# A diffusion backbone step on one core: the first feed-forward's way down by half products, two conditioning vectors moved to TensorE, and x added in the middle sweeps

## The chip, the cores and the metric

The kernel runs on 1 core of one Trainium2 chip. The metric is device microseconds of that core; the median of 3 runs before the change is 2879.01 us (2872.47 to 2881.43).

## What is computed

One layer of a hybrid backbone, for 1024 latent tokens and 128 context tokens with the same weights. All tensors are float32.

```python
def trunk_layer(x, mod, cache, lb, norm_g, ffn1, ffn2, mixer_w):
    m = [mod[:, i][:, None, :] for i in range(N_MOD)]
    x = x + 0.5 * m[2] * swiglu(modulate(x, norm_g[0], m[0], m[1]), *ffn1)
    mix, ctx = token_mixer(modulate(x, norm_g[1], m[3], m[4]), cache, lb, *mixer_w)
    x = x + m[5] * mix
    x = x + 0.5 * m[8] * swiglu(modulate(x, norm_g[2], m[6], m[7]), *ffn2)
    return x, ctx
```

`swiglu(h, w1, w3, w2)` is `(silu(h @ w1) * (h @ w3)) @ w2`, with 1024 model columns and 2816 hidden ones. The token mixer runs attention (8 heads) and a two-way scan side by side. The nine vectors `m` come from `silu(c) @ w_ada + b_ada`, one row for the latent tokens and one for the context; after the change `m[6]` and `m[7]` (shift and scale of the second feed-forward) are computed in another place.

## The kernel before, in words

**Layout.** The 1152 tokens lie along the free axis, the model's columns as 8 tiles `x[0..7]` of 128 x 1152, the hidden columns as 22 blocks `f` of 128. A float32 product is made of three matmuls in a rounded format: every operand is split into a high and a low part, ACT casts the high part, DVE or POOL subtracts to get the low one, and `hi*hi + hi*lo + lo*hi` is summed in PSUM (`mm3`, lines 473 to 475).

**Order of the stages.** Start; first way up (4 plain blocks, then 18 fast blocks); first way down; scan; attention; merge; second way up (3 plain blocks, 19 fast ones); second way down with the final norm. Instructions are issued in the order in which the generators are pulled, and a scheduler then orders each engine's queue. DMAs are issued by SP, in order.

**Fast blocks** (`fast_block`, L1746 its matmuls) compute a block of the way up with seven half-size products instead of eight, 288 tokens wide. Per block there are 2 x 7 x 4 x 3 = 168 matmuls. In them `ada_sum` works in the background: it computes vectors of `m` on DVE (L318), from a weight tile and a row broadcast over the partitions, vectors 2 to 5 in the first way up and 8 in the second.

**First way down** (`ffn_fast` with l = 0). The 22 hidden blocks are read back from HBM (`hs`), split into `hh` and `hl`, and multiplied two at a time: `down_group` (matmuls in `down`, L473 to L475, 384 tokens wide; L502 adds the scaled result to `x`), and the last four in `down_last`, which also starts the next norm. `x` was loaded before. In the background, `self.bg` runs `ada_sum` for the vectors 6 and 7, 64 DVE products in all.

**Second way down** (l = 1, `down_fast`). Sixteen hidden blocks are taken as 8 pairs in three groups of 2, 3 and 3 pairs. In the fast blocks `pair_sums` (L1783 to L1786) has made the seven sums of each pair and written them to HBM (`xd`), and `pair_weights` has made the sums of the weights on POOL and written them to `wsum`, for all but the last three sweeps. A group runs four sweeps `m` (`down_sweep`, L1946 its matmuls, 288 tokens wide); a sweep makes seven products in the order `PRODUCTS`, each for two halves of the tokens: 84 matmuls with two pairs, 126 with three. `down_ops` loads the weights, sums them where `own` holds (L1879, on POOL: four instructions, with the results `ws` twice, `raw` and `wr`), and splits them (ACT L1884, DVE L1885, tiles `wd`), six products ahead. `down_xs` loads the sums of the next group (`xr`, SP L1900, five raw tiles in flight) and splits them (ACT L1910; the low part, L1911, on DVE for the second pair and on POOL for the others) into tiles `xd`; it is pulled in the last sweep of the group before, one group of tiles per product. PSUM is drained by DVE into `su` (L1951) and `x` (L1931, L1933) and by ACT. The first group writes `x` afresh; in each sweep of the second and third group one tile of the old `x` is loaded and added by DVE in two halves (L1991).

**Attention** (`heads`, `block`) runs 16 blocks of nine key tiles. The PSUM tag `mx` (two banks) holds row maxima (L1411, L1412), queries, keys and values.

**Start.** `ada_pe` computes the vectors 0 and 1 on TensorE: per 128 rows of weights four matmuls, each 32 columns of the array wide, side by side (L263), then two transposes (L278).

Of the kernel before, what the change touches and what calls it, by code (L numbers as in the profile page):

```python
# [32 lines left out]
G = 32  # L33
# [12 lines left out]
GROUPS = (3, 2), (7, 3), (13, 3)  # L46
# [47 lines left out]
class Trunk:  # L94
# [27 lines left out]
    def start(self):  # L122
        nc, a, pp = self.nc, self.a, self.pp
        self.sc = self.fp.tile([P, KT, 32], F32, name="sc")
# [130 lines left out]
    def ada_pe(self, m, buf, pin=lambda i: i):  # L255
# [20 lines left out]
        pt = self.pp.tile([P, 2, P], F32, tag="ps1", bufs=1, name="adat")  # L276
# [8 lines left out]
        self.ada_end(m)  # L285

# [344 lines left out]
    def mixer_consts(self):  # L631
        nc, a, cp = self.nc, self.a, self.cp
        self.mask = cp.tile([P, 4, G], U8, name="mask")
        mf = self.tt(F32, "maskf")[:, : 4 * G]
        nc.sync.dma_start(mf, a["mask"])
        nc.vector.tensor_copy(self.mask.rearrange("p a b -> p (a b)"), mf)
# [3 lines left out]
        nc.vector.memset(self.onesb[64:128, 64:128], 1.0 / 64)  # L640
        self.onesq = cp.tile([P, P], F32, name="onesq")
# [490 lines left out]
    def heads(self, qn, ck, ckc, KT_, ktc, rope, w0, sums):  # L1132
# [36 lines left out]
        clear_v(Vs[1])  # L1169
        self.pend, self.mo = [], [None] * 8  # L1170
        pre = self.preload()
        for h in range(H):
# [19 lines left out]
        for _ in pre:  # L1192
# [599 lines left out]
    def pair_weights(self, w2):  # L1792

        nc = self.nc
        self.wsum = self.dp.tile([sum(n for _, n in GROUPS), P, KT // 2, 4, P], F32, name="wsum")
        n = sum(n for _, n in GROUPS)
        for j in range(n):
            f = GROUPS[0][0] + 2 * j
# [18 lines left out]
    def down_ops(self, w2):  # L1817
# [8 lines left out]
        def load(u, key):  # L1826
# [3 lines left out]
            j, f = sum(v for _, v in GROUPS[:g]), GROUPS[g][0]  # L1830
            own = g == len(GROUPS) - 1 and m > 0
# [28 lines left out]
        for u, (g, n, m) in enumerate(units):  # L1860
            load(u + 1, 6)
            load(u + 1, 2)
            if g == len(GROUPS) - 1 and m:
                a11, a21, a12, a22 = [nxt[u, i] for i in (6, 7, 2, 4)]
                s1, s2 = [
                    self.fp.tile([P, CW], F32, tag="hf", bufs=self.hfb, name="ws").rearrange("p (k d) -> p k d", k=n)
# [23 lines left out]
    def down_xs(self, g, X):  # L1890

        nc = self.nc
        j0 = sum(n for _, n in GROUPS[:g])
# [73 lines left out]
    def down_fast(self, w2, X, xg, ops, made, load_x, load_h, split_h, gm, nxt):  # L1967

        S = [self.tt(F32, "su")[:, :T].rearrange("p (m n) -> p m n", m=4) for _ in range(2)]
        rest = [2, *range(PLAIN[1] + 16, NF)]  # L1970
        pend, ws = [], []
        self.folds = []
        for g, (f, n) in enumerate(GROUPS):
            new = {} if g else X
            last = g == len(GROUPS) - 1
            for m in range(KT // 2):
# [38 lines left out]
        assert not self.folds  # L2015
        self.down_group(w2, fs, hs, gm, ws)
# [5 lines left out]
    def ffn_fast(self, l, gm, nxt):  # L2022
# [5 lines left out]
        self.puts, self.ticks, self.roles = [], 0, {}  # L2028
        if l:
# [256 lines left out]
```

## Time and profile before

| | |
|---|---|
| median of 3 runs | 2879.01 us |
| the profiled execution | 2879.34 us |
| its span | 2877.4 us |
| PE busy | 2781.1 us (97%) |
| DVE busy | 2026.9 us (70%) |
| ACT busy | 1332.1 us (46%) |
| POOL busy | 967.3 us (34%) |
| HBM traffic | 331.76 MB, 115 GB/s |

PE is TensorE's matmuls, PEld its weight loads, DVE VectorE, ACT ScalarE, POOL GpSimd, SP the queue that issues DMAs. Times in rows are microseconds from the span's start, a mean or a median marked ns is of one instruction. A row of a group of instructions ends with the idle time of the engine ahead of them and what ended it; a row of waits has the total, the number and the longest. In a row of stretches each engine has its busy time and, in brackets, its number of instructions; then come TensorE's granted clock as a share, the DMA engines' busy share and GB/s.

### The profile page before, as it was taken

Reading aid. Unit: us, or ns where it says so; the run is one execution under the profiler, and the core shown is the slowest. Engines: PE = TensorE matmul, PEld = TensorE weight load, DVE = VectorE, ACT = ScalarE, POOL = GpSimd, SP = SyncE. Lnnn points to the kernel's source line nnn. Section 1 sums busy time; section 2 is a strip of 40 time slices with the busy share of each in tenths; the row PEclk is TensorE's granted clock in tenths of the full one; section 3 lists DMA queues with packets and bytes.
Section 4 is the critical chain, followed back from the end, with each engine's and each line's share of the span. In section 5 each row is a group of like instructions: output and inputs, shape, how many; then the busy total and the mean of one; then the engine's idle time right before and its main releaser. Section 6 shows DMA issues by size and latency. Waiting matters only on the chain. (4 is left out here: it accounts for less than half of the span.)

```text
span 2877.4 us, 55665 instructions
## 1 busy us (share of the span) xinstructions
PE 2781.1 (97%) x21138; PEld 2642.6 (92%) x21138; DVE 2026.9 (70%) x4425; ACT 1332.1 (46%) x2738; POOL 967.3 (34%) x1005
## 2 busy tenths in 40 slices
PE   6999999999999999999999999989999999999998
PEld 5999999999999998988998787779989999999997
DVE  7677777577778777877355777756675666558885
ACT  6432322321166677667535777730552222236332
POOL 0133233354222222222144444532452433424450
PEclk9999999999999999999999999999999999999999
DMA  6644343663121111112412001262553443447631
GB/s 237 203 148 128 125 124 117 214 208 118 61 84 55 50 57 37 57 41 74 162 58 84 18 14 30 72 219 84 178 172 97 157 147 126 134 144 212 198 102 67
DMA packets 218941, 331.76 MB, mean 115 GB/s; under 512 B 24049, under 2 KB 142769, under 8 KB 218673
## 3 DMA queue, kind: packets, MB, share of 16 engines
q1 hardware_dynamic: 218672, 328.20, 35.4%
q8 instruction: 167, 2.74, 0.4%
q14 instruction: 102, 0.83, 0.1%
HBM read 244.93 MB, written 83.18 MB: 114 GB/s over the span
## 5 line engine op out<-in xcount | busy, mean ns | idle before, releaser
L1746 PE MATMUL b<-xo,wo 128*128 128x288 f32 x3552 | 482.0, 295 | 0.0
L1746 PEld LDWEIGHTS b<-xo,wo 128*128 128x128 f32 x3552 | 474.3, 188 | 0.0
L1746 PE MATMUL b<-bh,wo 128*128 128x288 f32 x1776 | 365.0, 295 | 1.2 <-ACT et L1756 1.2
L473 PE MATMUL mm<-xh,wh 128*128 128x384 f32 (+1 forms) x1008 | 351.8, 349 | 10.9 <-DVE sg L750 6.1
L474 PE MATMUL mm<-xl,wh 128*128 128x384 f32 (+1 forms) x1008 | 341.9, 339 | 0.0
L475 PE MATMUL mm<-xh,wl 128*128 128x384 f32 (+1 forms) x1008 | 341.4, 339 | 0.0
L1746 PEld LDWEIGHTS b<-bh,wo 128*128 128x128 f32 x1776 | 288.6, 188 | 1.4 <-ACT et L1756 1.4
L502 DVE SCALAR_TENSOR_TENSOR x<-dn,modt,x 128x256 f32<-128x256 f32 (+4 forms) x472 | 225.6, 499 | 86.9 <-PE dn L475 86.2
L1746 PE MATMUL b<-bl,wo 128*128 128x288 f32 x888 | 261.4, 294 | 0.0
L473 PEld LDWEIGHTS mm<-xh,wh 128*128 128x128 f32 (+1 forms) x1008 | 189.6, 188 | 21.0 <-DVE sg L750 8.3
L1720 ACT CAST wo<-raw 128x512 fp32r<-128x512 f32 x185 | 114.9, 622 | 180.1 <-issue 77.2
L474 PEld LDWEIGHTS mm<-xl,wh 128*128 128x128 f32 (+1 forms) x1008 | 189.3, 188 | 2.3 <-issue 0.7
L475 PEld LDWEIGHTS mm<-xh,wl 128*128 128x128 f32 (+1 forms) x1008 | 189.1, 188 | 1.0
L1946 PE MATMUL d<-xd,wd 128*128 128x288 f32 x1344 | 181.8, 297 | 7.4 <-DVE x L1933 5.4
L1946 PEld LDWEIGHTS d<-xd,wd 128*128 128x128 f32 x1344 | 180.0, 190 | 9.0 <-ACT wd L1884 3.6
L1721 DVE TENSOR_TENSOR wo<-raw,wo 128x512 fp32r<-128x512 f32 x185 | 128.4, 695 | 64.5 <-ACT wo L1720 61.8
L318 DVE SCALAR_TENSOR_TENSOR junk<-wada,cb 128x512 bf16<-128x512 f32 x224 | 163.4, 729 | 12.6 <-DMA wada<-in_w_aT 11.8
L1461 POOL TENSOR_TENSOR ehl<-e,ehl 128x512 fp32r<-128x512 f32 x93 | 122.1, 1317 | 140.6 <-ACT ehl L1459 75.8
L1746 PEld LDWEIGHTS b<-bl,wo 128*128 128x128 f32 x888 | 167.0, 188 | 0.0
L247 POOL TENSOR_TENSOR wl<-raw,wh 128x1024 fp32r<-128x1024 f32 (+3 forms) x51 | 101.2, 1986 | 174.3 <-ACT wh L246 162.3
L1721 DVE TENSOR_TENSOR wo<-ws,wo 128x512 fp32r<-128x512 f32 x74 | 71.2, 962 | 113.4 <-ACT wo L1720 113.2
L1720 ACT CAST wo<-ws 128x512 fp32r<-128x512 f32 x74 | 45.7, 618 | 227.5 <-POOL ws L1716 227.3
(441 smaller groups left out, 7202.6 us busy)
## 6 DMA issues: line engine op xcount, KB each, us to landing
raw<-in_w SPq DMA_DIRECT2D x148, 256.0 KB, 3.5
wada<-in_w_aT SPq DMA_DIRECT2D x112, 256.0 KB, 3.2
raw<-in_w SPq DMA_DIRECT2D x42, 512.0 KB, 4.0
raw<-in_w_in SPq DMA_DIRECT2D x41, 512.0 KB, 3.5
xr<-xd SPq DMA_DIRECT2D x56, 288.0 KB, 3.7
hr<-hs SPq DMA_DIRECT2D x26, 576.0 KB, 5.9
hb<-hd SPq DMA_DIRECT2D x44, 288.0 KB, 3.4
hs<-et SPq DMA_DIRECT2D x84, 144.0 KB, 2.2
```

The source lines that it names most:

```text
L247: pin((eng or self.nc.gpsimd).tensor_sub(wl, raw, wh))
L318: nc.vector.scalar_tensor_tensor(junk, ws[n % 2], 1.0, cs[s], ALU.mult, ALU.mult, accum_out=o)
L473: pin(nc.tensor.matmul(ps, wh, xh, start=start and i == 0, stop=False))
L474: pin(nc.tensor.matmul(ps, wh, xl, start=False, stop=False))
L475: pin(nc.tensor.matmul(ps, wl, xh, start=False, stop=stop and i == n - 1))
L502: nc.vector.scalar_tensor_tensor(self.x[m][:, a:b], ps[:, a - lo : b - lo], self.modt[:, gm, m, s : s + 1], self.x[m][:, a:b], ALU.mult, A ...
L1461: eng.tensor_sub(el, e, eh)
L1720: nc.scalar.copy(wh, src[i])
L1721: nc.vector.tensor_sub(wl, src[i], wh)
L1746: nc.tensor.matmul(ps, w[:, k], x[:, k, :QW], start=first, stop=last, skip_group_check=home != i)
L1946: nc.tensor.matmul(ps, w[:, k], xv, start=start, stop=stop, skip_group_check=home != i)
```

## The change

The first way down goes through `down_fast` too, with the first of its pairs at hidden block 4 (`self.plain`); the groups are now given from there. So the first way up makes the pair sums for 16 blocks and writes them as `xd` instead of `hs`. No `pair_weights` runs for it: `early` makes every sweep of the first way down sum its own weights on POOL. Blocks 0 to 3, 20 and 21 are still multiplied plainly, behind the groups. The vectors 6 and 7 are no longer computed by `ada_sum` in the first way down, but by a new `ada_fill` in attention, two rows of weights at a time: 8 matmuls into an `mx` bank, summed by DVE, and two transposes per vector; it is pulled at two places of each block from the second head on. In both ways down, the old `x` is loaded and added two tiles per sweep, in the code of the second and third sweep of the second and third group; the scheduler puts some of it ahead of them. The constants of the mixer are made in the second group of the first way down, and `sc`, the operand of the conditioning products, moves to a pool that lives through the kernel.

```diff
-GROUPS = (3, 2), (7, 3), (13, 3)
+GROUPS = (0, 2), (4, 3), (10, 3)
+PAIRED = 16
...
+    def ada_fill(self):
+
+        nc, a = self.nc, self.a
+        for m in (6, 7):
+            acc = self.fp.tile([P, 256], F32, tag="ada", bufs=1, name="adar")
+            for k in range(0, KT, 2):
+                w = [self.tt(F32, "wada")[:, :D] for _ in range(2)]
+                for i in range(2):
+                    nc.sync.dma_start(w[i], a["w_ada"][(k + i) * P : (k + i + 1) * P, m * D : (m + 1) * D])
+                yield
+                ps = self.pp.tile([P, 256], F32, tag="mx", bufs=2, name="adap")
+                for i in range(2):
+                    for g in range(4):
+                        v = slice(32 * g, 32 * g + 32)
+                        nc.tensor.matmul(
+                            ps[v, :],
+                            self.sc[:, k + i, :],
+                            w[i][:, 256 * g : 256 * g + 256],
...
+                if k:
+                    nc.vector.tensor_add(acc, ps, acc)
+                else:
+                    nc.vector.tensor_copy(acc, ps)
+                yield
+            self.ada_turn(m, acc, "mx", 2)
+            yield
...
+                    if h and t in (3, 7):
+                        next(fill, None)
...
-    def down_ops(self, w2):
+    def down_ops(self, w2, early):
...
-            own = g == len(GROUPS) - 1 and m > 0
+            own = early or (g == len(GROUPS) - 1 and m > 0)
...
-        rest = [2, *range(PLAIN[1] + 16, NF)]
+        rest = [*range(2, self.plain), *range(self.plain + PAIRED, NF)]
...
-                if g:
-                    xa.append((4 * g - 4 + m, load_x(4 * g - 4 + m)))
+                if g == 1 and m:
+                    next(consts, None)
+                if g and m in (1, 2):
+                    xa += [(i, load_x(i)) for i in range(4 * g + 2 * m - 6, 4 * g + 2 * m - 4)]
...
-                    if xa and k == 3:
-                        i, t = xa.pop()
+                    if xa and k in (2, 5):
+                        i, t = xa.pop(0)
...
-        dops, dmade, X = (self.down_ops(w2) if l else None), [], {}
-        xg = self.down_xs(0, X) if l else None
+        dops, dmade, X = self.down_ops(w2, l == 0), [], {}
+        xg = self.down_xs(0, X)
...
-            self.bg = self.ada_sum((6, 7), lambda: self.bank("up", "cb", D // 2), partial(self.tt, F32), self.slim)
-        if l:
-            self.down_fast(w2, X, xg, dops, dmade, load_x, load_h, split_h, gm, nxt)
-            return
-        for f in range(2, NF):
-            pend.append(split_h(*load_h(f)))
-            if f % 2 and f < NF - 1:
-                fs, hs = zip(*pend[:2])
-                self.down_group(w2, fs, hs, gm, ws or [load_w2(v) for v in fs])
-                pend, ws = pend[2:], None
-        for _ in self.bg:
-            pass
-        fs, hs = zip(*pend)
-        self.down_last(w2, fs, hs, gm, nxt)
+        self.down_fast(w2, X, xg, dops, dmade, load_x, load_h, split_h, gm, nxt)
```

Three places show how the engines' queues move. Line numbers in the rows of the changed kernel are its own; "128x576" is a shape, and "x25" behind it means 25 such instructions in a row.

POOL, where the second way down before the change goes from its first group over the second to the third (the splits `xd` of all three groups stand in these rows):

```order
L1716 TENSOR_TENSOR raw<-raw,ws 128x256 x2
L1911 TENSOR_TENSOR xd<-xr,xd 128x576 x25
L1879 TENSOR_TENSOR ws<-raw,wr 128x384
L1879 TENSOR_TENSOR raw<-raw 128x384
L1911 TENSOR_TENSOR xd<-xr,xd 128x576 x6
```

And POOL in the first way down of the changed kernel, at the change from the first group to the second (L1954 is the split, L1922 the sum of weights):

```order
L1954 TENSOR_TENSOR xd<-xr,xd 128x576
L1922 TENSOR_TENSOR ws<-ws,raw 128x384
L1954 TENSOR_TENSOR xd<-xr,xd 128x576
L1922 TENSOR_TENSOR wr<-wr,ws 128x256
L1922 TENSOR_TENSOR ws<-raw,wr 128x384
L1954 TENSOR_TENSOR xd<-xr,xd 128x576
L1922 TENSOR_TENSOR raw<-raw 128x384
L1954 TENSOR_TENSOR xd<-xr,xd 128x576 x5
L1922 TENSOR_TENSOR ws<-ws,raw 128x384
L1954 TENSOR_TENSOR xd<-xr,xd 128x576 x2
L1922 TENSOR_TENSOR wr<-wr,ws 128x384
L1954 TENSOR_TENSOR xd<-xr,xd 128x576 x4
```

Before, 14 splits of that change of groups stand in an unbroken row; now six sums stand among the 14. At the next change four sums stand among the splits where three stood.

PE in attention before the change, in the fourth pass of row maxima (`mtr` turns them, `po` are the products with the values, `sps` the scores):

```order
L1418 MATMUL mtr<-ident,m_18845 1x128 x4
L1428 MATMUL po<-ehl,V 128x512
L1429 MATMUL po<-ehl,V 128x512
L1430 MATMUL po<-ehl,V 128x512
L1452 MATMUL sps<-qh_17836,kth_17721 128x512
```

And the same place in the changed kernel:

```order
L1459 MATMUL mtr<-ident,m_19381 1x128 x4
L1469 MATMUL po<-ehl,V 128x512
L1470 MATMUL po<-ehl,V 128x512
L1471 MATMUL po<-ehl,V 128x512
L306 MATMUL adap<-wada,sc 32x256 x8
L1493 MATMUL sps<-qh_18367,kth_18252 128x512
```

Eight conditioning matmuls now stand between two key tiles; there are eight such places.

DVE in the second way down, first sweep of the third group, before the change (`x_29906` and `x_29905` are two tiles of x, `d` a PSUM bank):

```order
L1885 TENSOR_TENSOR wd<-ws,wd 128x384
L1933 SCALAR_TENSOR_TENSOR x_29906<-d_31794,modt,x_29906 128x288
L1991 TENSOR_TENSOR x_29906<-x_31706,x_29906 128x576
L1933 SCALAR_TENSOR_TENSOR x_29906<-d_31805,modt,x_29906 128x288
L1885 TENSOR_TENSOR wd<-raw,wd 128x384
L1991 TENSOR_TENSOR x_29906<-x_31706,x_29906 128x576
```

And in the same sweep of the changed kernel (`x_30560` and `x_30559` are the same two tiles of x, L1928 splits weights, L1976 drains PSUM into x, L2037 adds the old x):

```order
L1928 TENSOR_TENSOR wd<-ws,wd 128x384
L1976 SCALAR_TENSOR_TENSOR x_30560<-d_32418,modt,x_30560 128x160
L1976 SCALAR_TENSOR_TENSOR x_30560<-d_32418,modt,x_30560 128x128
L2037 TENSOR_TENSOR x_30560<-x_32549,x_30560 128x576
L1976 SCALAR_TENSOR_TENSOR x_30560<-d_32429,modt,x_30560 128x288
L1928 TENSOR_TENSOR wd<-wr,wd 128x384
L1976 SCALAR_TENSOR_TENSOR x_30560<-d_32396,modt,x_30560 128x288
L1976 SCALAR_TENSOR_TENSOR x_30559<-d_32446,modt,x_30559 128x288
L2037 TENSOR_TENSOR x_30560<-x_32549,x_30560 128x576
```

Before, the two halves stood between the drains of the sweep's fourth product; now they stand between those of its sixth. Of the group's other three tiles of old x, one is added at the end of the second sweep and two in the third; before, one was added in each of the last three sweeps.

More of the change, by code (lines that the diff above doesn't have):

```diff
@@ L275, in ada_pe, with ada_turn @@
         nc.scalar.copy(row, ps)
-        pt = self.pp.tile([P, 2, P], F32, tag="ps1", bufs=1, name="adat")
+        self.ada_turn(m, row, "ps1", 1)
+    def ada_turn(self, m, row, tag, bufs):
+        nc = self.nc
+        pt = self.pp.tile([P, 2, P], F32, tag=tag, bufs=bufs, name="adat")
         for q in range(2):
@@ L1794, in pair_weights @@
         nc = self.nc
-        self.wsum = self.dp.tile([sum(n for _, n in GROUPS), P, KT // 2, 4, P], F32, name="wsum")
-        n = sum(n for _, n in GROUPS)
+        n = PAIRED // 2
+        self.wsum = self.dp.tile([n, P, KT // 2, 4, P], F32, name="wsum")
         for j in range(n):
-            f = GROUPS[0][0] + 2 * j
+            f = self.plain + 2 * j
             for m in range(KT // 2 if j < n - GROUPS[-1][1] else 1):
@@ L1892, in down_xs @@
         nc = self.nc
-        j0 = sum(n for _, n in GROUPS[:g])
+        j0 = GROUPS[g][0] // 2
         units = [(i, k) for i in PRODUCTS for k in range(GROUPS[g][1])]
@@ L2015, in down_fast @@
         assert not self.folds
+        for _ in consts:
+            pass
         self.down_group(w2, fs, hs, gm, ws)
@@ L2027, in ffn_fast @@
         self.hs = self.dp.tile([NF, P, T], F32, name=f"hs{l}")
-        self.puts, self.ticks, self.roles = [], 0, {}
-        if l:
-            self.xd = self.dp.tile([sum(n for _, n in GROUPS), P, 7, 2, QW], F32, name="xd")
-            self.roles = {f + v: (j, v % 2) for j, f in enumerate(range(GROUPS[0][0], PLAIN[1] + 16, 2)) for v in range(2)}
+        self.puts, self.ticks, self.bg = [], 0, iter(())
+        self.plain = plain
+        self.xd = self.dp.tile([PAIRED // 2, P, 7, 2, QW], F32, name="xd")
+        self.roles = {plain + f: (f // 2, f % 2) for f in range(PAIRED)}
         sums, ops, made = iter(()), iter(()), []
```

49 lines of the change are left out of this document (20 added, 29 removed).

## The prediction

> **What bounds the kernel now.** The page comes first: who is busy, and at what clock.
>
> ```profile
> span 2877.4 us, 55665 instructions
> PE 2781.1 (97%) x21138; PEld 2642.6 (92%) x21138; DVE 2026.9 (70%) x4425; ACT 1332.1 (46%) x2738; POOL 967.3 (34%) x1005
> ...
> PEclk9999999999999999999999999999999999999999
> ```
>
> TensorE is busy for 97% of the span at almost the full clock. So a matmul taken away counts fully where PE runs without a gap, and a matmul added counts fully there too; work on the other engines counts only where PE waits for it. The next view is busy time by stage, because the change touches four stages: the fast blocks on the way up, both ways down, and attention.
>
> ```profile
> core 0: us, PE busy (x) PEld busy (x) DVE busy (x) ACT busy (x) POOL busy (x), PEclk, DMA share, GB/s
> 180.00:540.00 360.00, 360.00 (x2720) 360.00 (x2720) 262.69 (x591) 109.43 (x217) 106.52 (x129) 1.00 0.40 126
> 560.00:780.00 220.00, 220.00 (x1255) 219.82 (x1254) 171.42 (x414) 41.15 (x40) 96.35 (x39) 1.00 0.42 147
> 600.00:660.00 60.00, 60.00 (x343) 60.00 (x343) 47.29 (x115) 15.46 (x15) 28.61 (x12) 1.00 0.44 149
> 1560.00:1800.00 240.00, 238.26 (x1153) 191.97 (x1152) 173.94 (x330) 185.34 (x354) 115.86 (x101) 1.00 0.08 22
> 2460.00:2520.00 60.00, 60.00 (x456) 60.00 (x455) 35.82 (x68) 16.82 (x36) 24.05 (x38) 1.00 0.38 119
> 2596.00:2785.00 189.00, 181.65 (x1347) 179.98 (x1346) 162.50 (x307) 82.58 (x166) 75.88 (x48) 0.99 0.59 182
> ```
>
> In order: first fast blocks, first way down (two rows), attention, second fast blocks, second way down by half products. The first way down never lets PE wait (220.00 of 220.00). The second does, with DVE busy 162.50 of 189. The counts give the prices: a 384-wide matmul takes 60/343 = 174.9 ns in a full stream, a 288-wide one 60/456 = 131.6 ns, which is the same per column. Attention is PE's as well, with 1.74 us of 240 left.
>
> **Part 1, the first way down: matmuls.** Sixteen of its 22 blocks become half products. They now cost 16 x 8 x 3 x 3 = 1152 wide matmuls, 201.5 us; then 7 x 4 x 8 x 2 x 3 = 1344 narrow ones, 176.8 us. That is **-24.7 us**, an eighth, if PE finds everything in time. The other six blocks stay as they are.
>
> By the Trainium skill (TensorE: Matmul & The Clock Gate, Back-to-back issue gap) a stream of loads and matmuls takes 81 ns per matmul at 128 columns and 131 ns at 512; a line through these (an estimate from that page) gives 102 ns at 288 and 114 ns at 384, so half products would cost 5 us more instead of saving 25. The rows disagree: 131.6 and 174.9 ns, and I go by them.
>
> **Part 2, the first way down: waits.** The second way down has the same groups (2, 3 and 3 pairs) and shows what the form costs.
>
> ```profile
> L1946 PE MATMUL d<-xd,wd x1344: 288/295/442, 2596.0 to 2784.8; 128*128 128x288 f32 x192
> ```
>
> ```profile
> PE d L1946 <- DVE x L1933: 5.4, 6, 2.0
> ```
>
> ```profile
> 2630.00:2650.00 20.00, 17.96 (x125) 17.75 (x124) 20.00 (x24) 16.04 (x33) 18.33 (x11) 0.91 0.81 257
> 2650.00:2700.00 50.00, 49.27 (x368) 48.66 (x367) 40.22 (x82) 14.50 (x28) 6.93 (x6) 1.00 0.64 194
> 2720.00:2740.00 20.00, 15.43 (x111) 14.57 (x111) 19.50 (x39) 5.31 (x12) 9.40 (x8) 1.00 0.65 208
> 2740.00:2770.00 30.00, 30.00 (x229) 30.00 (x228) 27.94 (x61) 7.51 (x14) 5.47 (x5) 1.00 0.29 89
> ```
>
> From the first start to the last, 2596.0 to 2784.8, and one matmul more are 189.0 us, 12.2 over the 176.8. In the windows 27, 12 and 41 matmuls are missing against 152, 380 and 152: 3.6, 1.6 and 5.4 us. The first and third lie where one group of pairs gives way to the next: 21 tiles of the next group must be split within one sweep, two thirds of them on POOL.
>
> ```profile
> L1911 POOL TENSOR_TENSOR xd<-xr,xd 128x576 fp32r<-128x576 f32 x32 | 54.2, 1720 | 80.9 <-ACT xd L1910 80.3 <-DMA xr<-xd 0.6
> ...
> L1879 POOL TENSOR_TENSOR raw<-raw 128x384 f32<-128x384 f32 x3 | 3.8, 1279 | 0.2
> L1879 POOL TENSOR_TENSOR ws<-ws,raw 128x384 f32<-128x384 f32 x3 | 3.6, 1194 | 7.8 <-DVE wd L1885 7.8
> L1879 POOL TENSOR_TENSOR ws<-raw,wr 128x384 f32<-128x384 f32 x3 | 3.2, 1079 | 10.0 <-DMA wr<-in_w 7.2 <-DVE x L1933 2.2 <-DVE wd L1885 0.5
> L1879 POOL TENSOR_TENSOR wr<-wr,ws 128x384 f32<-128x384 f32 x3 | 3.1, 1018 | 16.3 <-issue 14.6 <-DVE wd L1885 1.7
> ```
>
> ```profile
> L1716 POOL TENSOR_TENSOR ws<-raw x74: 730/740/1632, 147.3 to 2560.8; 128x256 f32<-128x256 f32 x74
> ```
>
> ```profile
> SPq L1900 <- POOL xd L1911: 29.7, 22, 4.3
> ```
>
> Fourteen splits are 14 x 1.72 = 24.1 us of POOL, against a sweep of 84 x 0.1316 = 11.1 us and the next of 16.6 us: it just fits. The last row is the way it reaches PE: SP waits for POOL to free a raw tile, its loads come late, ACT's casts stand behind the late tile, and with them the weights.
>
> In the first way down the weight sums stand in this queue as well. A set for three pairs is 1.28 + 1.19 + 1.08 + 1.02 = 4.57 us, for two pairs 4 x 0.74 = 2.96 us; four sets and eight make 48.4 us where the second way has three sets, 13.7 us. At the first change of groups six sums (five of 384, one of 256: 6.5 us) now stand among the 14 splits, where the second way has none. Behind each wait splits, SP's loads and ACT's casts. PE stays whole if weights made six products ahead cover it (0), or loses all 6.5. POOL's 30.6 us against 27.7 us of sweeps puts it in between: I take 4. At the second change four sums (4.6 us) stand where three stood (3.6): +1, with 0 to 3 as ends. The first way's waits are so 12.2 + 4 + 1 = 17.2 us before Part 3.
>
> The sums can also hold up DVE:
>
> ```profile
> 2638.87 1.75 DVE L1885 TENSOR_TENSOR wd<-raw,wd 128x384 fp32r<-128x384 f32 x1
> ...
> 2655.92 0.54 DVE L1885 TENSOR_TENSOR wd<-raw,wd 128x384 fp32r<-128x384 f32 x1
> ```
>
> The same subtraction took 1.75 us beside a busy POOL and 0.54 us with POOL idle. If each of the 34.7 us of added sums held DVE back for its whole length, the 26.5 us that DVE has free in 189 would be overdrawn by 8 us. It is the far end; the sums are spread over sweeps and most DVE work reads PSUM, so I take 0. The Trainium skill (SBUF — State Buffer, Who interferes with whom) says that a DVE instruction with two SBUF inputs and a GpSimd instruction that reads SBUF exclude each other for a whole instruction, while one SBUF input is free of it. By that rule the far end is the case in which every sum meets such an instruction; the two rows agree with it.
>
> **Part 3, x in the middle sweeps, both ways down.** In DVE's queue the first tile of the third group moves from the fourth to the sixth product of its sweep, and of the last two tiles one moves into the third sweep beside the other, out of the fourth.
>
> ```profile
> DVE x L1991 <- DMA x<-xs: 4.3, 3, 2.8
> ```
>
> ```profile
> 2729.28 1.02 DVE L1991 TENSOR_TENSOR x<-x,x 128x576 f32<-128x576 f32 x1
> ...
> 2731.12 0.75 DVE L1991 TENSOR_TENSOR x<-x,x 128x576 f32<-128x576 f32 x1
> ```
>
> The 4.3 us in which DVE stood before a late x are the 1.6 us of PE in 2650:2700; with the loads a sweep later they should go, -1.6. The two adds at 2729 and 2731 (1.8 us) stand inside the worst wait, with DVE the engine that PE waits for; two products later DVE is still behind, so I count half, -0.9. Against this, the third sweep takes a second tile where DVE has 2.06 us left in 30 (2740:2770): 1.5 us more in 16.6 us overdraws it by 0.4. Together -2.1, with the ends -3.4 (the adds go in full) and +3 (two adds of 1.5 us move a wait nowhere and make one of their own). I take **-2 per way down**. The mask of the mixer, cast in the same sweeps now, is one DVE instruction of 0.2 us and nothing waits for it there:
>
> ```profile
> L636 DVE CAST mask<-maskf 128x128 uint8<-128x128 f32 x1 | 0.2, 226 | 0.8 <-DMA maskf<-in_mask 0.8
> ```
>
> **Part 4, two vectors in attention.** The start of the kernel runs the same products between narrow matmuls.
>
> ```profile
> 50.64 0.29 PE L475 MATMUL ps<-bh,wl 128*128 128x288 f32 x1
> 50.87 1.07 PE L263 MATMUL adap<-wada,sc 128*32 128x256 f32 x16
> 51.87 0.40 PE L473 MATMUL ps<-bh,wh 128*128 128x288 f32 x1
> 52.10 0.30 PE L474 MATMUL ps<-bl,wh 128*128 128x288 f32 x1
> ```
>
> ```profile
> 33.80 0.56 PE L278 MATMUL adat<-ident,adar 128*128 128x128 f32 x2 [0.49 <-ACT adar L275]
> ```
>
> ```profile
> PE qps L473 <- DVE mx L1412: 1.7, 5, 0.6
> ```
>
> Between the starts at 50.64 and 52.10 lie two narrow matmuls (0.26) and 1.20 us for two rows of weights. Eight such steps are 9.6 us, and two pairs of transposes 0.2 to 0.56 us each, say 0.8 in all. Each step also takes one of the two `mx` banks until DVE has read it; such a wait was 0.6 us at most and 0.34 on average (1.7/5), so 0 to 4.8 us: I take 1. Attention has no room for it: **+11.4**. The 16 loads of 512 KB go out on SP with DMA at 0.08.
>
> Taken away are 64 DVE products and 32 loads of 256 KB from the first way down. PE waited for nothing there, so that is 0.
>
> **Part 5, the fast blocks of the first way up** get pair sums as the second has:
>
> ```profile
> L1786 DVE TENSOR_TENSOR hp<-et 128x288 f32<-128x288 f32 x16 | 7.3, 456 | 0.3
> ```
>
> Eight subtractions per pair are 3.6 us in two blocks (2 x 168 x 0.1316 = 44.2 us), beside a DVE at 262.69 of 360, 73%: 81% then. What hides it is PE's own work, 0; without that cover 3 us. The six writes of a pair replace four on SP at a DMA share of 0.40.
>
> **The sum.** -24.7 + 17.2 - 2 (first way down) - 2 (second) + 11.4 = -0.1 us. Against the profiled execution, 2879.34 us (span 2877.4, 1.9 around it), that is 2879.2. It lies 0.3 over the median of the runs, 2879.01, so nothing has to be shifted.
>
> **The rivals.**
> *POOL sets the first way down* (slower). The 6.5 and the 3 us come in full, DVE is overdrawn by 8 us, and x gives nothing in either way: waits of 12.2 + 17.5 = 29.7, and -24.7 + 29.7 + 11.4 = +16.4: 2896. It decides from waits of 22 us on. For it speak POOL's 30.6 us against 27.7, and a DVE at 162.50 of 189; against it that weights are made six products ahead.
> *The sums find gaps* (faster). POOL is idle for 113 us of the second way down's 189. If the sums cost nothing, x brings 3.4 in each way and the steps in attention 9.6: -24.7 + 12.2 - 6.8 + 9.6 = -9.7: 2870.
> *Attention hides the vectors* (the addition costs nothing): -24.7 + 15.2 - 2 = -11.5: 2868. Against it speaks 238.26 of 240.
>
> **How the numbers follow.** What a measurement of this kernel can tell from no change is about 0.3%, 8.6 us. My forecast, within that, has 0.57 (its own range 2871 to 2888); the slower rival 0.30, since the unknown costs pile up on that side; the two faster ones 0.11 and 0.02. The range goes from 2866, a little under the faster rivals, to 2896.
>
> **What would show it.** Right: the first way down's half products span about 192 us (176.8 + 15.2), with missing matmuls where the groups change; the second way's about 187; attention's PE time 10 to 12 us longer; fast blocks still without gaps. Wrong: half products over 198 us, POOL or ACT named in PE's waits (POOL rival); under 186 (gaps); attention no longer (third rival); gaps between 180 and 540 us (Part 5).

## The result, and the profile after

| | before | after |
|---|---|---|
| median of 22 runs each | 2877.96 us | 2880.81 us |
| ratio, 95% interval | | 1.0013 (1.0007 to 1.0019) |
| the profiled execution | 2879.34 us | 2876.97 us |
| its span | 2877.4 us | 2875.2 us |

The change costs about 3 us, 0.1%: real by its interval, and under the 0.3% that the prediction set as its bound. The two profiled executions stand the other way round (2.4 us less after), since the one of after is the fastest of its 22 runs. So the two spans aren't compared as wholes; stages are, beside how much a stage moves that nobody touched. The merge and the plain blocks behind it took 279.0 us in this profile, and 280.4 to 286.5 in the other thirteen.

The page's first lines of after:

```profile
span 2875.2 us, 56736 instructions
PE 2766.5 (96%) x21462; PEld 2622.4 (91%) x21462; DVE 2062.8 (72%) x4420; ACT 1376.9 (48%) x2876; POOL 993.6 (35%) x1058
```

PE has 324 matmuls more (192 in the first way down, the rest in attention), and 14.6 us less to do. Busy time by stage, after: first fast blocks (the same 360 us as shown of before), the first way's half products, attention, the second way's half products:

```profile
180.00:540.00 360.00, 360.00 (x2720) 360.00 (x2720) 284.29 (x655) 106.41 (x218) 107.63 (x130) 1.00 0.45 145
553.10:751.10 198.00, 184.88 (x1346) 182.60 (x1345) 166.06 (x308) 82.82 (x168) 112.29 (x82) 0.97 0.50 153
1557.50:1892.20 334.70, 324.81 (x1600) 250.66 (x1599) 246.21 (x455) 252.78 (x483) 156.48 (x129) 0.99 0.22 66
2594.90:2783.00 188.10, 179.79 (x1346) 178.42 (x1345) 159.00 (x306) 83.81 (x167) 77.05 (x49) 1.00 0.59 183
```

And attention before, from its first scores to the merge:

```profile
1566.50:1891.20 324.70, 315.37 (x1467) 247.10 (x1466) 242.03 (x444) 252.88 (x483) 156.36 (x129) 0.99 0.15 42
```

Fast blocks: PE still whole, DVE from 262.69 to 284.29; from first to last matmul they took 401.9 us before and 402.4 after. The first way's half products: 198.0 us, 21.2 over the 176.8 of their matmuls. Attention: 10.0 longer. Second way: 188.1 for 189.0. From the first way's start to the mixer's first matmul the profiles have 287.0 us before and 280.2 after, -6.8. The touched stages add up to -6.8 + 0.5 + 10.0 - 0.9 = **+2.8 us**, which is what the medians say. That it fits this closely is luck: the second way alone took 187.3 to 190.9 us in profiles in which nothing of it was changed.

What PE waited for in the first way's half products, and where. The rows of 20, 40 and 30 us are the start, the first change of groups and the second; a full stream has 152, 304 and 228 matmuls there.

```profile
PE d L1989 <- DVE mask L673: 4.5, 1, 4.5
PE d L1989 <- DVE x L1976: 4.1, 3, 2.6
PE d L1989 <- DVE su L1994: 1.9, 1, 1.9
PE d L1989 <- ACT x L1972: 1.3, 1, 1.3
```

```profile
553.10:573.10 20.00, 18.57 (x135) 17.66 (x134) 16.69 (x36) 8.88 (x25) 8.48 (x10) 1.00 0.69 205
593.10:633.10 40.00, 33.32 (x228) 32.67 (x227) 33.31 (x53) 18.37 (x37) 29.74 (x20) 0.91 0.70 220
683.10:713.10 30.00, 24.99 (x173) 24.27 (x172) 28.63 (x56) 7.79 (x15) 14.85 (x12) 0.94 0.57 176
```

The same three places in the second way down of before:

```profile
2596.00:2616.00 20.00, 20.00 (x153) 19.99 (x152) 14.92 (x38) 10.05 (x28) 0.00 (x0) 1.00 0.81 230
2636.00:2676.00 40.00, 37.43 (x267) 36.83 (x267) 35.59 (x58) 16.82 (x34) 17.86 (x11) 0.96 0.84 264
2716.00:2746.00 30.00, 25.43 (x187) 24.57 (x186) 28.71 (x55) 9.31 (x18) 14.86 (x12) 1.00 0.59 184
```

Missing are 17, 76 and 55 matmuls, against 0, 37 and 41. The 70 more are 9.2 us, which is the difference between 21.2 and 12.2. At the first change POOL is busy 29.74 of 40 us, where it was 17.86. The third place is the least sure of the three: in the second ways of all fourteen profiles (120 to 150 us behind their start) 41 to 57 matmuls are missing, and the first way's 55 lie inside that.

The worst wait is dearer than it looks. Windows of after around it:

```profile
615.00:620.00 5.00, 0.68 (x3) 0.71 (x4) 5.00 (x8) 2.27 (x6) 3.33 (x2) 0.84 0.80 247
620.00:622.00 2.00, 2.00 (x10) 2.00 (x10) 2.00 (x7) 0.00 (x0) 0.77 (x1) 0.50 0.88 269
622.00:624.00 2.00, 2.00 (x10) 2.00 (x9) 1.52 (x5) 0.00 (x0) 1.92 (x3) 0.50 1.00 372
624.00:626.00 2.00, 2.00 (x12) 2.00 (x12) 1.32 (x3) 0.51 (x1) 1.50 (x2) 0.69 0.99 285
626.00:628.00 2.00, 2.00 (x17) 2.00 (x16) 1.97 (x4) 0.51 (x1) 0.31 (x1) 1.00 0.81 302
```

After 4.5 us without work the granted clock is 0.50; PE is busy without a gap, and makes 10 matmuls in 2 us and not the later 17. It is back at 1.00 some 6 us on. The Trainium skill (TensorE: Matmul & The Clock Gate, Part 1: The HAM clock gate) says that the clock goes to half after an idle window of some 3.4 us and needs as much sustained work to come back; the trace agrees on the half, and has it last some 6 us here.

### The profile page after: what moved, and what is told of

Same layout as the page of the kernel before. It is cut to its first block, busy times and chain, and to the rows that moved or that the text cites. A ratio compares the mean times of both kernels' runs of the same rounds, so it can differ in the third digit from the quotient of the medians.

```text
span 2875.2 us, 56736 instructions
## 1 busy us (share of the span) xinstructions
PE 2766.5 (96%) x21462; PEld 2622.4 (91%) x21462; DVE 2062.8 (72%) x4420; ACT 1376.9 (48%) x2876; POOL 993.6 (35%) x1058
## 5 line engine op out<-in xcount | busy, mean ns | idle before, releaser
L1989 PE MATMUL d<-xd,wd 128*128 128x288 f32 x2688 | 365.1, 298 | 21.4 <-DVE x L1976 7.0
L1989 PEld LDWEIGHTS d<-xd,wd 128*128 128x128 f32 x2688 | 361.3, 190 | 25.1 <-issue 6.7
L509 PEld LDWEIGHTS mm<-xh,wh 128*128 128x128 f32 (+1 forms) x1008 | 189.1, 188 | 20.8 <-DVE sg L788 7.3
L1954 POOL TENSOR_TENSOR xd<-xr,xd 128x576 fp32r<-128x576 f32 x70 | 119.2, 1727 | 98.7 <-ACT xd L1953 94.6
L1757 POOL TENSOR_TENSOR ws<-raw 128x256 f32<-128x256 f32 x74 | 62.8, 869 | 241.1 <-DMA raw<-in_w 210.3
L509 PE MATMUL ps<-bh,wh 128*128 128x288 f32 (+1 forms) x448 | 135.6, 304 | 4.5 <-DVE sl L1717 2.8
```

What stands on the lines that cost most here:

```text
L509: pin(nc.tensor.matmul(ps, wh, xh, start=start and i == 0, stop=False))
L1757: nc.gpsimd.tensor_tensor(o[:, c], x[:, c], y[:, c], op)
L1954: (nc.vector if k == 1 else nc.gpsimd).tensor_sub(lo, raw, hi)
L1989: nc.tensor.matmul(ps, w[:, k], xv, start=start, stop=stop, skip_group_check=home != i)
```

## The experiments

Half products and fast blocks are given from the first to the last start of their matmuls; times are medians, ratios are to the kernel before in the same runs.

### Weight sums made early: all, eight sets, ten sets

All sums of the first way ahead of it:

```diff
-        sums = self.pair_weights(w2) if l else iter(())
-        dops, dmade, X = self.down_ops(w2, l == 0), [], {}
+        sums = self.pair_weights(w2)
+        dops, dmade, X = self.down_ops(w2, False), [], {}
```

> The weight sums of the first way down are made in the fast blocks before it, as for the second way, and written to HBM; only three of its twelve sweeps still sum on POOL. Theory (the sums among POOL's splits are what the first way's half products, 198.0 us, lose over the second way's 188.1): its half products span 188 to 191 us, POOL's burst at the first change of groups shrinks from about 32 us to 25, and the time falls by 7 to 10 us, to about 2872. Rival (the sums are not the cause; the splits alone overload the change of groups, and the first way differs from the second by its loads or by DVE): the span stays at 196 to 198 and the time within 2 us. In the fast blocks POOL is 30% busy, so 0 there; if DVE is held up by POOL there, the blocks lengthen beyond 402.4 us.

Measured: 2901.23 us, 1.0089 (1.0076 to 1.0101). The half products did what the theory said:

```profile
L1989 PE MATMUL d<-xd,wd x1344: 288/295/603, 580.8 to 770.6; 128*128 128x288 f32 x192
```

189.8 us for 197.9. But the fast blocks took 430.9 us for 402.4. Two waits of DVE and SP in them (160 to 540), and one of POOL, that were small or absent in after:

```profile
DVE junk L354 <- DMA wada<-in_w_aT: 40.5, 13, 6.0
```

```profile
SPq L1854 <- POOL wq L1851: 40.1, 15, 5.3
```

```profile
POOL wq L1849 <- DMA wq<-in_w: 102.6, 15, 12.4
```

DVE's was 14.1 us in after; it suggested that late conditioning weights stop DVE. The next two runs asked that, and how few sums would do.

Eight sets only, and their steps at two products of a block:

```diff
+HEAD = (0, 3), (1, 0), (2, 0)
...
-            own = early or (g == len(GROUPS) - 1 and m > 0)
+            own = (early and (g, m) not in HEAD) or (g == len(GROUPS) - 1 and m > 0)
...
-                if n != 3:
+                if n != 3 if l else n in (3, 6):
                     next(sums, None)
```

> Only the sums of the three sweeps at the changes of groups in the first way (fourth sweep of the first group, first sweeps of the second and third: 8 of 23 sets of pairs) are made in the fast blocks, two steps per block, in products where no conditioning product is issued. Theory (the sums among the splits are the cost; and the fast blocks of the run with all sums early lost 28.5 us because SP's queue, stopped by sums, brings the conditioning weights late to a DVE that waits for them in order): half products of the first way 190 to 193 us against 197.9, fast blocks 402 to 406, time 2874 to 2879. Rival (POOL sums beside DVE in the fast blocks cost by their own length): fast blocks 402.4 plus 8/23 of 28.5, 412 us, and the time 2884 or more.

Measured: 2877.78 us, 1.0000 (0.9991 to 1.0008); fast blocks 404.5, half products 196.8. The cost in the fast blocks is small, so the rival there falls; the gain is small too, against the theory's 190 to 193. At the three places (windows laid as above, from the start of the half products) 18, 54 and 59 matmuls are missing, for 17, 76 and 55: only the first change gained. The second did not, although the sums of its first sweep had been moved. POOL at the first change shows what is left there: three sums still stand among the splits, those of the next sweep.

```profile
592.56 6.58 POOL L1955 TENSOR_TENSOR xd<-xr,xd 128x576 fp32r<-128x576 f32 x4 [1.66 <-ACT xd L1954]
599.63 1.01 POOL L1923 TENSOR_TENSOR ws<-raw,wr 128x384 f32<-128x384 f32 x1 [0.50 <-DVE wd L1929]
600.59 1.93 POOL L1955 TENSOR_TENSOR xd<-xr,xd 128x576 fp32r<-128x576 f32 x1
602.49 1.31 POOL L1923 TENSOR_TENSOR raw<-raw 128x384 f32<-128x384 f32 x1
603.76 3.69 POOL L1955 TENSOR_TENSOR xd<-xr,xd 128x576 fp32r<-128x576 f32 x2
607.95 1.02 POOL L1923 TENSOR_TENSOR ws<-ws,raw 128x384 f32<-128x384 f32 x1 [0.50 <-DVE wd L1929]
608.93 10.93 POOL L1955 TENSOR_TENSOR xd<-xr,xd 128x576 fp32r<-128x576 f32 x6
```

All sums early, with the conditioning weights three steps ahead:

```diff
-        ws = [w2[:, :HD], w2[:, HD : 2 * HD]]
+        ws = [t[:, s] for t in (w2("wada"), w2("wada")) for s in (slice(HD), slice(HD, 2 * HD))]
...
-            if n + 1 < len(units):
-                load(n + 1)
+            if n + 3 < len(units):
+                load(n + 3)
```

> All sums early, as in the first run, but the conditioning products of the fast blocks have their weights loaded three steps ahead and not one. Theory (late conditioning weights, 40.5 us of DVE waiting in the first run against 14.1 in the changed kernel, are what stops DVE and so PE): the fast blocks fall from 430.9 to 402 to 408 us, half products stay at 190, time 2872 to 2880. Rival (SP's queue itself, that stands 40 us before writes of sums, delays the weights of the blocks and the writes of the pairs, or POOL slows DVE): fast blocks stay over 420 and the time over 2893.

Measured: 2898.38 us, 1.0073 (1.0060 to 1.0085); fast blocks 426.2, half products 188.3. DVE's wait for conditioning weights is gone (0.3 us), and the loss stays: this theory falls.

```profile
DVE junk L354 <- DMA wada<-in_w_aT: 0.3, 1, 0.3
```

```profile
POOL wq L1849 <- DMA wq<-in_w: 83.8, 14, 12.4
```

What the traces still have: PE waits for the blocks' Silu on ACT, 14.6 us here and 1.8 in after. POOL stands 83.8 us for the loads of the pairs' weights, with the blocks' own weight sums (L1757) behind it in the same queue. But in after POOL stands longer for its own loads, and the blocks lose nothing, so that wait alone does not explain the loss. In this run, then in after:

```profile
PE b L1787 <- ACT et L1797: 14.6, 9, 4.5
```

```profile
PE b L1787 <- ACT et L1797: 1.8, 1, 1.8
POOL ws L1757 <- DMA raw<-in_w: 150.5, 17, 12.8
```

What holds the blocks up with all sums early stays open. What is shown is how to avoid it: with few sums, put where no conditioning product is issued, the blocks stay at 403 to 405 us. Number and place were changed together, and no run tells which of the two does it.

Ten sets, those of the sweeps in which matmuls were missing:

```diff
+HEAD = (0, 0), (0, 3), (1, 0), (1, 1)
...
-                if n != 3:
+                if n != 3 if l else n in (3, 5, 6):
                     next(sums, None)
```

> Ten sets of sums are made in the fast blocks: those of the first and fourth sweep of the first group and of the first and second sweep of the second. Theory (what is lost is lost at the transition from the fast blocks and at the first change of groups; the first wants the sums of the first sweep gone, the second those of the second group's first two sweeps, of which the eight early sets left one): the start of the half products loses 5 matmuls and not 16, the first change about 27 and not 71; half products 190 to 193 us, the fast blocks 402 to 407, time 2873 to 2879. Rival (with a few sums gone the waits only move on, as the second change of groups grew in the run with eight): half products 195 us or more, time 2879 or more.

Measured: **2875.87 us**, 0.9989 (0.9980 to 0.9997); fast blocks 403.2, half products 189.1.

```profile
553.30:573.30 20.00, 19.74 (x149) 19.50 (x148) 16.05 (x35) 9.45 (x27) 4.98 (x6) 1.00 0.56 167
593.30:633.30 40.00, 36.51 (x272) 35.89 (x271) 35.93 (x58) 17.74 (x36) 20.95 (x15) 1.00 0.75 237
673.30:703.30 30.00, 26.72 (x186) 26.07 (x185) 28.65 (x58) 8.88 (x18) 17.00 (x13) 0.94 0.59 183
```

Missing are 3, 32 and 42 matmuls for 17, 76 and 55 (the third window starts 10 us earlier than in after, as the sweeps in it do), and POOL is busy 20.95 of the 40 us for 29.74. Three later runs have the same ten sets, beside other edits far from here: their half products took 191.2, 192.9 and 193.0 us, with 7 to 9, 24 to 38 and 65 to 67 missing. In the six profiles that have all sums in place it is 17 to 23 at the start and 67 to 78 at the first change, for half products of 197.9 to 199.9 us. So the sums among the splits of the first change, and those at the transition from the fast blocks, are what the first way lost there. Moving them is worth 5 to 9 us; 189.1 is the best of four. At the second change, whose sums were left, the four together gained nothing. This version beats both kernels, the one before by 0.1%, with an interval that ends at 0.9997.

### The mask back ahead of the first way down

```diff
-        consts = self.mixer_consts() if nxt == 1 else iter(())
+        consts = iter(())
...
+        if not l:
+            for _ in self.mixer_consts():
+                pass
         self.down_fast(w2, X, xg, dops, dmade, load_x, load_h, split_h, gm, nxt)
```

> The mixer's mask and constants are made ahead of the first way down, as before the change. The profile names the cast of the mask on DVE as what ended PE's longest wait, 4.46 us at 619. Theory (the cast of 0.21 us only stands in DVE's queue beside what PE waited for; before it stood two weight subtractions of 1.39 and 1.75 us beside a busy POOL, and 2 us of waiting for ACT): the wait stays at 4 us or more, put down to another line, and the time changes by less than 1 us. Rival (the mask's transfer or cast is the cause): the wait goes, half products of the first way span about 191 to 193.5, and the time falls by 4.5 to 7 us, the clock's dip behind the wait included.

Measured: 2882.16 us, 1.0017 (1.0008 to 1.0026); half products 199.9 us. The time is 1.4 us over the changed kernel's, for the less than 1 that was expected, and the intervals overlap. The longest wait is as long as it was, 4.5 us, now under another name:

```profile
PE d L1989 <- DVE x L1976: 8.2, 4, 4.5
```

So the mask's was that of a neighbour. DVE's queue in after, up to the end of PE's wait at 619.33, shows what stood there:

```profile
614.46 0.94 DVE L1954 TENSOR_TENSOR xd<-xr,xd 128x576 fp32r<-128x576 f32 x1 [1.99 <-ACT xd L1953]
...
615.69 1.39 DVE L1928 TENSOR_TENSOR wd<-wr,wd 128x384 fp32r<-128x384 f32 x1
617.00 1.75 DVE L1928 TENSOR_TENSOR wd<-raw,wd 128x384 fp32r<-128x384 f32 x1
618.67 0.51 DVE L1976 SCALAR_TENSOR_TENSOR x<-d,modt,x 128x288 f32<-128x288 f32 x1
619.10 0.21 DVE L673 CAST mask<-maskf 128x128 uint8<-128x128 f32 x1
```

The drain at 618.67 frees a PSUM bank; ahead of it are two weight subtractions, of 1.39 and 1.75 us beside a busy POOL (0.54 with POOL idle), and a split that waited 1.99 us for ACT. No run tells these two apart.

### x one tile per sweep, as before

```diff
-                if g and m in (1, 2):
-                    xa += [(i, load_x(i)) for i in range(4 * g + 2 * m - 6, 4 * g + 2 * m - 4)]
+                if g:
+                    xa.append((4 * g - 4 + m, load_x(4 * g - 4 + m)))
...
-                    if xa and k in (2, 5):
-                        i, t = xa.pop(0)
+                    if xa and k == 3:
+                        i, t = xa.pop()
```

> The old x is loaded and added one tile per sweep in all sweeps of the second and third group, as before the change. Theory (Part 3 of the prediction): the second way's half products go from 188.1 back to 189 to 190 us and the first way's from 198.0 to about 200; the time rises by 2 to 4 us. Rival (the place of the adds is worth nothing; waits only move): each way within 0.7 us of what it was, and the time within 1 us; with its other end, that two adds in one sweep cost more than they bring, the first way's falls to 196 or less.

Measured: 2882.94 us, 1.0019 (1.0010 to 1.0027). First way 198.8 us, second 190.8. The second fits the theory's 189 to 190, but the same second way took 187.3 to 190.9 us in profiles in which nothing of it was changed, and the first way's 198.8 lies inside its own 197.9 to 198.9. The interval of the time overlaps that of the changed kernel. Inconclusive: the place of the adds is worth too little to be seen here.

### The two vectors: left out, on DVE in attention, on DVE ahead of it

Left out:

```diff
-        fill = self.ada_fill()
+        fill = iter(())
+        nc.vector.memset(self.modt[:, 6:8], 0.0)
+        self.ada_end(7)
```

> The two conditioning vectors are left out (zeros stand for them), so attention has no such matmuls, loads or transposes; everything else is as in the changed kernel. Theory (PE is what attention waits for, so each step adds its whole PE time): attention from its first scores to the end goes from 334.7 to 324 to 325 us, and the time falls by 9 to 11 us. Rival (part of the 10 us is noise of one profile or lies beside waits): the time falls by 3 to 6 us.

Measured: 2869.78 us, 0.9973 (0.9964 to 0.9982), 11.0 us under the changed kernel; attention 323.5 us for 334.7. TensorE pays for the vectors in full.

On DVE, inside attention:

```diff
-        fill = self.ada_fill()
+        fill = self.ada_late()
...
-                    if h and t in (3, 7):
+                    if h and t in (0, 2, 4, 6, 8):
                         next(fill, None)
```

(`ada_late` runs `ada_sum` for the vectors 6 and 7 with its tiles in attention's pools.)

> The two vectors are still computed in attention, but on DVE, as products of a weight tile with a row that is broadcast over the partitions, 64 instructions of about 0.74 us (their mean in the first fast blocks) from the second head on; TensorE does nothing for them. DVE is busy 246 of attention's 335 us, so 47 us more make 293 of 325. Theory (PE is attention's bound, DVE has room): attention from its first scores falls back to 325 to 328 us and the time to 2871 to 2874. Rival (DVE serves row maxima and PSUM in order, and a 0.74 us product in front of them, or one that waits for its weights, stops PE, as may be the case in the fast blocks of the run with early sums): attention stays at 332 us or more, the time is 2879 or more.

Measured: 2955.98 us, 1.0271 (1.0257 to 1.0284); attention 408.0 us. The rival's side, by far more than 47 us of products can explain. The next run moved the products out of attention, `next(fill)` being called where the queries, keys and values are made:

> The two vectors are computed on DVE again, 64 products, but ahead of attention, in the stretch in which the end of the scan and attention's first queries, keys and values are made (1400 to 1566 in the changed kernel; DVE busy 90 of 166 us, PE 161). Theory (a DVE product costs nothing where PE has long streams of matmuls ahead of it that do not ask DVE for each; attention is different, since there PE waits for a row maximum after each product): the stretch grows by 0 to 4 us, attention falls back to 325, the time to 2869 to 2875, which beats both kernels. Rival (47 us more on a DVE that serves in order, beside 16 to 32 loads of 256 KB, hold up the norms of this stretch as they hold up the row maxima): the stretch grows by 10 us or more and the time is 2880 or more.

Measured: 2955.35 us, 1.0259 (1.0240 to 1.0277). The first scores came 31.7 us later (1589.2 for 1557.5), but attention, with no DVE product in it, still took 375.0 us. So DVE's products were only a part of it. ACT's groups in that attention show what else is new:

```profile
L1493 ACT ACT_TABLE_LOAD x16 | 20.5, 1283 | 0.3
L1494 ACT ACT_TABLE_LOAD x13 | 16.7, 1283 | 0.2
```

With two more at the Exp of the scores (L1513) that is 31 loads; in the run without the vectors attention has none. `ada_sum` applies Silu to the conditioning rows. That replaced the table that held Ln and Exp together, and from then on each block loaded one table for its Ln and one for its Exp (L1493 and L1494 here). ACT's order, in the run with the products in attention, shows it (L1485 is the Ln, L1486 the Exp); the next block has the same rows from 1629.82 on:

```profile
1604.12 1.28 ACT L1485 ACT_TABLE_LOAD   x1
1605.42 0.59 ACT L1485 ACTIVATE rc<-po 64x512 f32<-64x512 f32 x1
1606.03 1.28 ACT L1486 ACT_TABLE_LOAD   x1
```

The Trainium skill (ScalarE: Activation LUTs, Table sets: the hidden batching unit) says that one set holds Ln and Exp together; the trace agrees, with no load in attention where that set stays. The 1283 ns for a load are the trace's.

Both edits together with the early sums:

> The two previous edits together. If they add: the changes of the two against the changed kernel's 2880.8 us summed, within 2 us; by the theories of both 2862 to 2871, faster than the kernel before by 0.3 to 0.5%. If the vectors' DVE work and the early sums meet nowhere, nothing else can come of it, since the stages lie 840 us apart.

Measured: 2943.93 us, 1.0232 (1.0216 to 1.0248). The two edits' changes, +74.5 and -4.9, make 2950.4; it came out 6.5 us lower, outside the 2 us that were expected; the four runs of the first of the two edits spread over 14 us.

Two runs put the table right, with ten early sums. First the products ahead of attention, Silu issued before the table of Ln and Exp is loaded:

```diff
+        self.fill = fill = self.ada_late()
+        next(fill)
         self.lnexp()
```

> Ten early sums, and the vectors on DVE ahead of attention, with the Silu of the conditioning rows issued before the table of Ln and Exp is loaded, so that attention keeps one table. Theory (the two runs with vectors on DVE lost 75 us mostly to ACT's table loads, two per block of attention at 1.28 us each, since the table of Silu had replaced the one that holds Ln and Exp together; attention with no DVE product in it was 39 us longer): attention falls back to 325 us, the stretch ahead of it keeps its own loss, up to 30 us in the run without early sums (its first scores came at 1589 for 1557) where DVE was busy 36 of 40 us; the time is 2870 to 2895. Rival (DVE's products are the loss, in both places): attention stays over 350 us, the time over 2930.

Measured: 2891.30 us, 1.0045 (1.0030 to 1.0059). Attention is back at 324.6 us; the stretch from the half products to the first scores is 831.7 us for 807.7 in the run with ten sums alone. DVE's products, with their loads, cost 24 us there.

Then inside attention, the table loaded again behind each Silu:

```diff
                 for s in range(2):
-                    nc.scalar.activation(cs[s], row[s], AF.Silu)
+                    self.tc.keep_in_program_order(nc.scalar.activation(cs[s], row[s], AF.Silu))
+                if cb:
+                    self.lnexp()
```

> Ten early sums, and the vectors on DVE inside attention, with the table of Ln and Exp loaded again behind each Silu (two loads more and not some forty). Theory (the table loads were the loss, and DVE, 246 of 335 us busy, has room for 47): attention from its first scores 326 to 332 us against 334.7 with the vectors on TensorE, time 2868 to 2874, faster than both kernels. Rival (a product of 0.74 us in front of a row maximum stops PE each time: 64 times a part of it, and late weights): attention 345 us or more, time over 2885. In between, each product costs a part of its length.

Measured: 2905.74 us, 1.0096 (1.0081 to 1.0112). Attention, and in it the vectors' products on DVE:

```profile
1551.20:1918.10 366.90, 328.42 (x1468) 249.22 (x1467) 308.74 (x577) 259.14 (x491) 167.46 (x129) 0.98 0.22 66
```

```profile
L365 DVE SCALAR_TENSOR_TENSOR junk<-wada,cb 128x512 bf16<-128x512 f32 x64 | 60.2, 941 | 0.6
```

366.9 us, with 4 table loads; 408.0 had 37 of them. 33 loads of 1.28 us are 42.3, the difference is 41.1. Ahead of attention it was 375.0 us with 31 loads (39.8 us) and 324.6 with none, so a load costs attention about its length there, or more. And the products, with these four loads (5.1 us), cost 42 us over an attention without vectors (324.7), though DVE is busy only 308.74 of 366.90. PE's waits for row maxima (`mx`, and `m` ahead of the turning) are a part of it, in this run and then in the one without vectors:

```profile
PE mps L1463 <- DVE mx L1464: 9.7, 17, 1.5
PE mtr L1470 <- DVE m L1467: 8.2, 7, 1.6
```

```profile
PE mps L1454 <- DVE mx L1455: 2.4, 5, 1.4
PE mtr L1461 <- DVE m L1458: 0.6, 1, 0.6
```

So the rival's mechanism holds without the table: these waits are 14.9 us longer, and PE's own busy time is 14.4 us longer (328.42 for 313.98). The remainder is in smaller waits. Where PE waits for row maxima, DVE's free time was no room.

## Why the prediction was right

The forecast, 2879.2 us and no measurable change, held: 2880.81. It held in part by luck, since the terms missed by more than the sum did. By the two profiles the first way's waits cost 6.0 us more than forecast (21.2 for 15.2), the second way gained 1.1 less and the fast blocks cost 0.5. Against these 7.6 us, the first way's other blocks gained 3.4 for which there was no term, and attention cost 1.4 less. Point by point:

- **Part 1** (-24.7): right. The half products are 1344 matmuls, and what is over 176.8 us is waits and clock.
- **Part 2** (waits of 12.2 + 4 + 1): the place was right, the size short. Against the second way the first lost 39 matmuls more at the first change (76 - 37), 5.1 us for the 4; 14 more at the second, 1.8 for the 1; and 17 at the transition from the fast blocks, 2.2 us, which had no term. The first and the last are shown to be the sums, since they went with ten sets made early (24 to 38 and 3 to 9 missing). The 14 are not: the second way itself varies that much there, and the run that moved sums of that place gained nothing at it. A wait of 4.5 us costs the half clock behind it as well. The path is shown in part: POOL's queue was put down as holding back splits, loads and casts, and a hold-up of DVE was put at 0; at the longest wait DVE's queue has both, a split that came 1.99 us late from ACT and two subtractions slowed beside POOL.
- **The bounds for the POOL rival**: 198.0 us stand on the prediction's sign of being wrong (over 198), and three other profiles with the same first way have 198.2 to 198.9. The 21.2 of waits stop just short of the 22 from which it would have decided, and ACT is named in one wait of 1.3 us. This rival was close.
- **Part 3** (-2 per way): not seen in either way. The run that undid it can't tell it from 0. The mask's cast costs nothing, as costed.
- **Part 4** (+11.4): right; 10.0 by the two profiles, 11.2 against the attention without vectors, 11.0 by the time.
- **Part 5** (0): right; 0.5 us, DVE at 79% for the 81% forecast.
- **Not in the sum**: the first way before had waits of its own and a little slower stream, at its start and near its end, outside the 220 us that the prediction read. Its last six blocks, up to the mixer's first matmul, are 82.2 us after the change, 6.6 over their 75.6; the way before was 10.0 over its 277.0. That is 3.4 us gained, so the first way came to -24.7 + 21.2 - 3.4 = -6.9 us for the forecast -9.5; the second way gave 0.9 for 2, within what it varies.
- **The rivals**: POOL, the slower one, had the right place and came to half of its price there (9.2 us of waits more than the second way, for 17.5). That sums find gaps was wrong as the kernel stands. With ten sets moved the first way came to 189.1 to 193.0 us, which is 12.3 to 16.2 of waits for the second way's 12.2. That attention hides the vectors was wrong.

## What to carry to other kernels

Work that is moved to an engine with free time is paid by where it stands in that engine's queue: eight sets of sums, those of the sweeps at the changes of groups, left the start as it was and three sums among the splits, and gained 1.1 us; ten sets, those of the sweeps where matmuls were missing, gained 5 to 9. Count missing matmuls by window rather than idle time, since they hold the half clock behind a wait too, and lay the windows at the same sweeps in both kernels. Before a function moves to ACT in a new stage, look which table that stage keeps.

## What the runs showed that was not expected

- A Silu ahead of attention brought 31 table loads into it and made it 50 us longer (375.0 for 324.6), since Ln and Exp no longer shared a table; with the Silu inside, 33 more loads cost 41 us.
- 64 DVE products of 0.94 us each, with four table loads, cost attention 42 us at a DVE that was busy 75% before; the same two vectors cost 10 us on TensorE, the engine that bounds it.
- A wait of 4.5 us was followed by some 6 us at half the granted clock.
- The releaser that a wait names can be a neighbour in the queue: moving the mask changed nothing.
